# Softmax times V: transposed probabilities copied out of PSUM two row blocks at a time, and the store of the second last pass moved between the loads of the last head

## Chip, cores, metric

One core of one Trainium2 chip. The metric is the device time of one execution in microseconds (us); lower is better. Medians are over the runs named.

## The reference

```python
batch, n_heads, seq, head_dim = 8, 12, 1024, 64        # float32
attn = np.exp(scores - scores.max(-1, keepdims=True))
attn = attn / (attn.sum(-1, keepdims=True) + 1e-8)
return np.matmul(attn, v)
```

There are 96 heads. Each has 4 MB of scores and needs 1024 x 1024 exponentials.

## The kernel before

The loop takes four heads (k = 0 to 3) per pass, 24 passes. A head is 8 row blocks (r) of 128 rows. For each two row blocks ScalarE takes exponentials (the kernel does not subtract the row's maximum first). Then, for each row block, TensorE transposes eight 128x128 squares into one PSUM tile, VectorE copies the tile to SBUF, and TensorE makes eight products with V and a column of ones. VectorE divides by the sums.

```python
EB = 2; LAG = 2; AHEAD = 4                   # row blocks per exponential, lag of products, heads per pass
p_bufs   = buffers(sb_pool, 8, [P, EB, SK], FP16, "p_nat")
pt_bufs  = buffers(sb_pool, 4, [P, SK], FP16, "pt")
psT_bufs = buffers(ps_pool, 4, [P, SK], FP16, "psT")
# ... cut ...
def heads(n0):
    for k in range(AHEAD):
        # ... cut: for k == 0, spread_v of this head ...
        for r in range(R):
            # ... cut: exponential of two row blocks when r is even (one by one at the very end) ...
            psT = take(psT_bufs)
            for c in range(C):
                nc.tensor.transpose(out=psT[:, c*P:(c+1)*P], in_=p_row[:, c//L, c%L, :], identity=order16[:])
            pt = take(pt_bufs)
            copy = nc.vector.tensor_copy(out=pt[:], in_=psT[:])
            # ... cut: on every other r spread_v of the next head; at r == R-1 load_next ...
            pending.append((n0, k, r, pt, st))
            if len(pending) > LAG:
                finish(pending.pop(0))       # eight products; then reciprocal and scaling (normalise)
    while pending:
        finish(pending.pop(0))
    cast_v()
    last(n0)                                 # loads of later heads and the store of heads 2 and 3
# in last(), for the pass before the last:
load(AHEAD - 2, BH - 2, (4, 4))
load(AHEAD - 1, BH - 1, (2, 2, 2, 1, 1))     # the very last head, in five parts
store(n0, AHEAD - T)
```

## Time and profile before

| | before |
|---|---|
| median of the first three runs | 1066.23 us |
| span in the profile | 1064.1 us |
| occupied: 16 DMA engines / VectorE / ScalarE / TensorE | 99.2% / 74% / 69% / 69% |
| DMA rate, 20 to 1000 us | 432 GB/s |
| last store issued / landed | 1059.60 / 1062.24 us |

The DMA engines are occupied nearly all the time and no compute engine above 74%, so over most of the run the data sets the time. Only near the end, as the loads run out, does compute count.

### The profile page before, as it was taken

To read this page: it belongs to the slowest core of one execution; us is meant where nothing else is said; L and a number is where in the kernel's file an instruction comes from. 1 tells how busy PE (TensorE), PEld (TensorE's weight loads), DVE (VectorE), ACT (ScalarE), POOL (GpSimd) and SP (SyncE) were. 2 spreads that over 40 slices of the span, in tenths; PEclk is the share of its full clock that TensorE was granted. 3 is DMA by queue.
4 is the path that set the end of the run, shared out by engine and by line. 5 is a ranking of instruction groups with operands and counts; after the bars stand their busy time and mean duration, and the time that the engine had idled before them with its cause. 6 is when DMAs were issued, how large, how long until landed. Compare 5 with 4: busy or idle time off the path is not lost.

```text
span 1064.1 us, 32213 instructions
## 1 busy us (share of the span) xinstructions
PE 734.8 (69%) x12288; PEld 682.6 (64%) x12288; DVE 786.6 (74%) x1589; ACT 735.8 (69%) x432; POOL 48.0 (5%) x31
## 2 busy tenths in 40 slices
PE   2766766767766667677686776767666777667675
PEld 2765765667666667666575665767665667666575
DVE  3776867868768777677786776868768687686777
ACT  3766776666767668586676866667766668676685
POOL 0000000000000000000000000000000000000000
PEclk9888888878889888888888888878889787897989
DMA  9999999999999999999999999999999999999995
GB/s 394 432 420 434 425 433 434 433 434 433 433 432 432 424 439 432 434 429 427 434 431 436 434 432 434 431 435 422 439 432 434 430 426 435 434 432 427 439 427 233
DMA packets 24915, 453.05 MB, mean 426 GB/s; under 512 B 2768, under 2 KB 2768, under 8 KB 9168
## 3 DMA queue, kind: packets, MB, share of 16 engines
q1 hardware_dynamic: 24912, 453.00, 99.2%
q8 instruction: 3, 0.05, 0.0%
HBM read 436.21 MB, written 25.17 MB: 434 GB/s over the span
## 4 chain that ended last, share of the span: by engine, by line
DMA 78%; ACT 13%; PEld 4%; PE 3%; DVE 1%; issue 1%; SPq 0%; ACTq 0%; DVEq 0%
DMA s_nat<-in_scores_dram 78%; ACT p_nat L255 13%; PEld L267 2%; PE psT L267 2%; PEld L145 1%; DVE pt L273 1%; PE psO_whole L145 1%; PE psO L145 1%; SPq L185 0%; DVE out_sb L129 0%; ACTq L255 0%; SPq L197 0%; DVE recip L124 0%; ACTq L227 0%; DVE vones L208 0%
## 5 line engine op out<-in xcount | busy, mean ns | idle before, releaser
L255 ACT ACTIVATE p_nat<-s_nat 128x2048 f16<-128x2048 f32 (+1 forms) x408 | 705.0, 1800 | 226.7 <-DMA s_nat<-in_scores_dram 200.9
L267 PE MATMUL psT<-order,p_nat 128*128 128x128 f16 x6144 | 578.0, 247 | 263.9 <-ACT p_nat L255 256.9
L273 DVE COPY pt<-psT 128x1024 f16<-128x1024 f16 x768 | 515.6, 687 | 199.9 <-PE L267 121.3
L267 PEld LDWEIGHTS <-p_nat 128*128 128x128 f16 x6144 | 449.9, 123 | 291.1 <-ACT p_nat L255 288.8
L145 PEld LDWEIGHTS <-pt 128*128 128x128 f16 x6144 | 303.1, 108 | 84.4 <-DVE pt L273 81.4
L145 PE MATMUL psO<-vones,pt 128*128 128x65 f16 x3072 | 177.9, 202 | 56.2 <-DVE pt L273 52.6
L145 PE MATMUL psO_whole<-vones,pt 128*128 128x65 f16 x3072 | 190.3, 212 | 3.3 <-DVE pt L273 2.9
L208 DVE COPY vones<-v_half 32x512 f16<-32x512 f16 x384 | 109.4, 285 | 23.1 <-POOL v_half L204 6.0
L255 ACT ACT_TABLE_LOAD x24 | 30.8, 1283 | 89.7 <-DMA s_nat<-in_scores_dram 81.7
L204 POOL CAST v_half<-v_sb 128x2048 f16<-128x2048 f32 x25 | 47.3, 1893 | 1002.2 <-DVE vones L208 957.1
L129 DVE TENSOR_TENSOR out_sb<-psO,recip 64x256 f32<-64x256 f32 x192 | 81.2, 423 | 6.1
L129 DVE TENSOR_TENSOR out_sb<-psO_whole,recip 64x512 f32<-64x512 f32 x96 | 66.1, 688 | 3.7 <-DMA out_dram<-out_sb 0.7
L124 DVE RECIPROCAL recip<-psO 128x4 f32<-128x4 f32 x96 | 17.1, 179 | 34.2 <-PE psO L145 17.8
L124 DVE RECIPROCAL recip<-psO_whole 128x8 f32<-128x8 f32 x48 | 9.7, 203 | 4.8 <-PE psT L267 4.0
L71 DVE MEMSET vones<- 128x16 f16 x4 | 0.2, 72 | 0.8 <-PEq L309 0.8
L62 DVE CAST order<-ident 128x128 f16<-128x128 f32 x1 | 0.2, 227 | 0.4 <-POOL ident masks.py:199 0.4
masks.py:199 POOL TENSOR_SCALAR_AFFINE_SELECT ident<-ident 128x128 f32<-128x128 f32 x1 | 0.3, 292 | 0.1
masks.py:197 POOL MEMSET ident<- 128x128 f32 x1 | 0.2, 204 | 0.3 <-POOLq L309 0.3
L309 POOL MEMSET const-float32-0.0<- 128x1 f32 x1 | 0.1, 98 | 0.2 <-issue 0.2
L309 POOL MEMSET const-bfloat16-1.0<- 128x1 bf16 x1 | 0.1, 102 | 0.0
L309 POOL MEMSET const-uint8-127<- 128x1 uint8 x1 | 0.1, 102 | 0.0
L309 POOL MEMSET const-float32-1.0<- 128x1 f32 x1 | 0.1, 98 | 0.0
## 6 DMA issues: line engine op xcount, KB each, us to landing
s_nat<-in_scores_dram SPq DMA_DIRECT2D x96, 4096.0 KB, 35.9
v_sb<-in_v_dram SPq DMA_DIRECT2D x24, 1024.0 KB, 33.0
out_dram<-out_sb SPq DMA_DIRECT2D x48, 512.0 KB, 27.0
s_nat<-in_scores_dram SPq DMA_DIRECT2D x2, 2048.0 KB, 32.8
s_nat<-in_scores_dram SPq DMA_DIRECT2D x3, 1024.0 KB, 32.6
s_nat<-in_scores_dram SPq DMA_DIRECT2D x2, 512.0 KB
```

Of the source, the lines that this page charges most:

```text
L62: nc.vector.tensor_copy(out=order16[:].rearrange("p (t j) -> p t j", t=T), in_=ident32[:].rearrange("p (j t) -> p t j", t=T),)
L71: nc.vector.memset(vo[:, :, D : D + 2], 1.0)
L124: nc.vector.reciprocal(out=recip, in_=psO[:, :, :, D : D + 1])
L129: nc.vector.tensor_tensor(out=rows.rearrange("j (b g) d -> j b g d", g=G), in0=psO[part, :, :, 0:D], in1=recip[part].to_broadcast([W, last ...
L145: nc.tensor.matmul(out=bank[:, g * M : (g + 1) * M], lhsT=pt[:, c * P : (c + 1) * P], rhs=st["vones"][:, c, 0:M], start=(c == 0), stop=(c ...
L204: nc.gpsimd.tensor_copy(out=v_half[:], in_=v_sb[:])
L208: copy = nc.vector.tensor_copy(out=vones_bufs[k][s * Q : (s + 1) * Q, :, 0:D].rearrange("i (h l) d -> i h l d", l=L), in_=v_half[k * Q : ( ...
L255: nc.scalar.activation(out=p_nat[:, g : g + rows, :].rearrange("p r (x v) -> p x r v", v=Q * L), in_=s_bufs[k][:, r + g : r + g + rows, :] ...
L267: nc.tensor.transpose(out=psT[:, c * P : (c + 1) * P], in_=p_row[:, c // L, c % L, :], identity=order16[:],)
L273: copy = nc.vector.tensor_copy(out=pt[:], in_=psT[:])
L309: nc = _bacc.Bacc("TRN2", target_bir_lowering=False, num_devices=1)
```

## The change

The intent is to halve the number of VectorE copies (a single one took 687 ns in the kernel before), and to have the store of the pass before land early, so that the last pass does not wait for it.

```diff
-    pt_bufs = buffers(sb_pool, 4, [P, SK], FP16, "pt")
+    pt_bufs = buffers(sb_pool, 2, [P, EB, SK], FP16, "pt")
-    psT_bufs = buffers(ps_pool, 4, [P, SK], FP16, "psT")
+    psT_bufs = buffers(ps_pool, 2, [P, EB, SK], FP16, "psT")
...
                 load(AHEAD - 2, BH - 2, (4, 4))
-                load(AHEAD - 1, BH - 1, (2, 2, 2, 1, 1))
+                load(AHEAD - 1, BH - 1, (4,))
                 store(n0, AHEAD - T)
+                load(AHEAD - 1, BH - 1, (2, 1, 1), 4)
...
                 if r % EB == 0:
-                    p_nat = take(p_bufs)
+                    p_nat, psT, pt = take(p_bufs), take(psT_bufs), take(pt_bufs)
...
-                        out=psT[:, c * P : (c + 1) * P],
+                        out=psT[:, r % EB, c * P : (c + 1) * P],
...
+                if k < AHEAD - 2 and r == R - 1:
+                    load_next(k, n0)
+                if r % EB < EB - 1:
+                    continue
                 copy = nc.vector.tensor_copy(out=pt[:], in_=psT[:])
-                if k < AHEAD - 1 and r % (R // S) == 0:
-                    spread_v(k + 1, r // (R // S), copy)
-                if r == R - 1:
-                    load_next(k, n0)
-                pending.append((n0, k, r, pt, st))
-                if len(pending) > LAG:
+                if k < AHEAD - 1:
+                    spread_v(k + 1, r // EB, copy)
+                pending.extend((n0, k, r - EB + 1 + e, pt[:, e], st) for e in range(EB))
+                while len(pending) > LAG:
                     finish(pending.pop(0))
```

More of the change, by code (lines that the diff above doesn't have):

```diff
@@ L179, in apart, with load @@
         )
-    def load(k, n, parts=(R,), **cond):
-        r = 0
+    def load(k, n, parts=(R,), r=0, **cond):
         for rows in parts:
@@ L264, in heads @@
                 p_row = p_nat[:, r % EB, :].rearrange("p (h q l) -> p h l q", q=P, l=L)
-                psT = take(psT_bufs)
                 for c in range(C):
                     nc.tensor.transpose(
-                        out=psT[:, c * P : (c + 1) * P],
+                        out=psT[:, r % EB, c * P : (c + 1) * P],
                         in_=p_row[:, c // L, c % L, :],
@@ L271, in heads @@
                     )
-                pt = take(pt_bufs)
+                if k < AHEAD - 2 and r == R - 1:
+                    load_next(k, n0)
+                if r % EB < EB - 1:
+                    continue
                 copy = nc.vector.tensor_copy(out=pt[:], in_=psT[:])
-                if k < AHEAD - 1 and r % (R // S) == 0:
-                    spread_v(k + 1, r // (R // S), copy)
-                if r == R - 1:
-                    load_next(k, n0)
-                pending.append((n0, k, r, pt, st))
-                if len(pending) > LAG:
+                if k < AHEAD - 1:
+                    spread_v(k + 1, r // EB, copy)
+                pending.extend((n0, k, r - EB + 1 + e, pt[:, e], st) for e in range(EB))
+                while len(pending) > LAG:
                     finish(pending.pop(0))
@@ L284, in heads @@
         last(n0)
-    assert BH % AHEAD == 0 and BH >= 2 * AHEAD and SK == Q * S * C
+    assert R // EB == S and BH % AHEAD == 0 and BH >= 2 * AHEAD and SK == Q * S * C
     load_v(0)
```

## The prediction

> **What bounds the kernel now.** I read the page's busy shares first, then the slices and the DMA section, then the chain, then the last 20 us in the timeline of VectorE.
>
> ```profile
> PE 734.8 (69%) x12288; PEld 682.6 (64%) x12288; DVE 786.6 (74%) x1589; ACT 735.8 (69%) x432; POOL 48.0 (5%) x31
> ...
> DMA  9999999999999999999999999999999999999995
> ...
> q1 hardware_dynamic: 24912, 453.00, 99.2%
> ...
> DMA 78%; ACT 13%; PEld 4%; PE 3%; DVE 1%; issue 1%; SPq 0%; ACTq 0%; DVEq 0%
> ```
>
> No compute engine is above 74%, while the 16 DMA engines are occupied for 99.2% of the span; only the last slice falls short. A table of windows gives a DMA share of 1.00 and 432 GB/s from 20 to 1000 us. One head moves 453 MB / 96 = 4.72 MB, which is 10.9 us at 432 GB/s. VectorE needs 786.6 / 96 = 8.2 us per head, PE and ScalarE 7.7 each. So VectorE has 2.7 us to spare on every head. The chain agrees: 78% of it is the load of scores. The only places where compute can set the time are the first loads, which the change leaves alone, and the end, after the DMA stream runs dry.
>
> ```profile
> 1048.73 1.89 DVE L273 COPY pt<-psT 128x1024 f16<-128x1024 f16 x3
> 1050.54 0.20 DVE L124 RECIPROCAL recip<-psO_whole 128x8 f32<-128x8 f32 x1
> 1050.70 0.69 DVE L273 COPY pt<-psT 128x1024 f16<-128x1024 f16 x1
> 1052.14 1.41 DVE L129 TENSOR_TENSOR out_sb<-psO_whole,recip 64x512 f32<-64x512 f32 x2 [0.74 <-DMA out_dram<-out_sb]
> 1053.57 1.89 DVE L273 COPY pt<-psT 128x1024 f16<-128x1024 f16 x3
> 1055.38 0.17 DVE L124 RECIPROCAL recip<-psO 128x4 f32<-128x4 f32 x1
> 1055.47 0.66 DVE L273 COPY pt<-psT 128x1024 f16<-128x1024 f16 x1
> 1056.16 0.88 DVE L129 TENSOR_TENSOR out_sb<-psO,recip 64x256 f32<-64x256 f32 x2
> 1057.07 0.69 DVE L273 COPY pt<-psT 128x1024 f16<-128x1024 f16 x1
> 1058.48 0.18 DVE L124 RECIPROCAL recip<-psO 128x4 f32<-128x4 f32 x1 [0.72 <-PE psO L145]
> 1058.70 0.88 DVE L129 TENSOR_TENSOR out_sb<-psO,recip 64x256 f32<-64x256 f32 x2
> ```
>
> This is the end. VectorE is nearly solid from 1048.7 to 1059.6, with two holes: 0.74 us waiting for a store, and 0.72 us waiting for the last product. The first hole is what the second half of the change aims at: normalising the head before the last overwrites an output buffer whose previous store is queued behind every load, so it lands only at 1052.1. The second belongs to the last link (last copy, eight products, reciprocal, scaling). The final store is then issued at 1059.60, lands 2.6 us later, and the span ends at 1064.1.
>
> ScalarE also matters here. In its timeline the last head's exponentials start at 1044.62 (rows 0,1), 1046.42 (2,3), 1048.40 (4,5), 1050.22 (6) and about 1051.2 (7), ending at 1052.22. Rows 4,5 were waiting for data:
>
> ```profile
> L185 SPq DMA_DIRECT2D s_nat<-in_scores_dram x1: 328/328/328, 1015.0 to 1015.0; - x1
> DMA to landing us min/median/max: 33.3/33.3/33.3
> ```
>
> Issued at 1015.0, landed at 1048.3, used at 1048.40. The transfers before it, read alike, landed at 1043.3 (rows 0,1) and 1045.8 (rows 2,3): 2.5 us per megabyte.
>
> [...] with the store last in the queue landing last; so a store placed earlier pushes back the loads behind it by its own transfer time. [...] The trace has 687 ns per copy and 0.65 us from start to start back to back[...] VectorE is saturated only in the last 10 us.
>
> **The change part by part.**
>
> *Copies.* 768 copies of 687 ns become 384 of twice the size. [...] 384 x 1.221 = 469 us against 515.6 in the by-form groups, and VectorE falls from 786.6 to about 740 us (70%). On the path in the steady state: nothing, because it adds to a slack of 2.7 us per head. PSUM stays at four row blocks, now as two pairs. The instruction order on PE becomes 16 transposes of the next pair, then 16 products of the pair before, so a copy has a whole group of products and transposes to hide behind. Coarser hand-off does not starve PE either: 7.7 us of work per head, and 10.9 us to do it in. Later release of a score buffer would cost nothing, since a load has some 36 us from issue to landing, more than three heads of queue.
>
> *Loads and store at the end.* The last head came as 2,2,2,1,1 rows, then the store. Now it is 4 rows, the store, then 2,1,1. The bytes are the same, so the last byte of the stream stays where it is, near 1051.7. But the pieces move: 0.5 MB of store is 1.25 us, half of the 2.5 above. Rows 0 to 3 land together at 1045.8 (rows 0,1 thus 2.5 us later than before); the store at about 1047.1 (it was 1052.1); rows 4,5 at 1049.55; row 6 at about 1050.8; row 7 at about 1052.1.
>
> *The end, step by step (us, on the old trace's axis).* ScalarE: rows 0,1 from 1045.93 (before: 1044.62), then 1.81 apart: 1047.75 for rows 2,3, 1049.64 for rows 4,5 (after their landing), 1051.45 for row 6, 1052.45 for row 7, ending at 1053.45, 1.2 later than before. VectorE, with 1.0 us for 16 transposes and the order that the built program has:
> - copy of rows 0,1: 1047.83 + 1.1 = 1048.95 to 1050.17;
> - reciprocal and scaling of the head before, 0.20 + 1.41, with no wait for the store: to 1051.8;
> - copy of rows 2,3 to 1053.0 (transposed long before);
> - copy of rows 4,5 to 1054.2;
> - reciprocal and scaling of the first bank, 0.18 + 0.88: to 1055.3;
> - copy of rows 6,7, whose transposes follow the products of rows 2,3 and end near 1054.8: 1055.35 to 1056.57;
> - 16 products instead of 8 before the end: 0.64 + 8 more at 0.03 = 0.90, to 1057.5;
> - reciprocal and scaling, 1.1: to 1058.63.
>
> Before, this point was 1059.58. The sum: four copies of 1.22 for eight of 0.67 saves 0.5; the store's wait saves 0.74; the later arrival of rows 0,1 makes VectorE begin this stretch some 0.3 later than its own backlog would, and the final 16 products cost 0.26 more. Together about -0.9 to -1.0. The final store and the close (4.5 us) are unchanged. So 1066.23 - 1.0 = **1065.2 us**, 0.1% faster.
>
> **The rivals.**
>
> *The store before the last rows simply delays the end.* If the last row's arrival bound the end, everything after ScalarE's last exponential (7.4 us in the trace, 1052.22 to 1059.60) would shift by 1.2, and the time would be about 1067.4. For it: rows 4,5 were waited for. Against it: in the trace VectorE, not ScalarE, is the solid engine after 1048.7, and when the last exponential ended it still had five copies and two scalings to do. I give it one chance in six, in part or whole.
>
> *VectorE was a hidden bound, and 46 us less of it shortens the run.* Its busiest slices show 8 tenths. If each head were gated by it, up to 0.5 us x 96 = 46 us, 4%, would come off. Against it: the DMA share of 1.00 through 980 us; time can only fall if DMA falls, and no byte is removed. Under 1%.
>
> *Two PSUM tiles turn into a new wait in every pair.* Four single buffers let PE run up to four blocks ahead; two pairs let it start the third pair only when the first is copied. If transposes and copies alternated strictly, a pair would cost about 16 transposes (1.3 at the granted clock of 0.84) plus 1.22 copy plus 0.29, then products 0.9: 3.7 us, 14.8 per head, above 10.9, and the run would be near 1400. The order of instructions rules out the strict form, because copies of one tile run beside transposes into the other. A partial form raises PE's idle time, and still has some 2 us per head to hide in. About 1% for anything over 2%.
>
> **Range and chances.** The repeats of before span 0.36 us. My step sum carries perhaps 0.6 either way (copy duration over two banks, order of arrival), the delay rival pulls up to 1.2 above before, and the DMA stream itself may drift by a tenth of a per cent between two programs. Hence 1064.0 to 1066.8. Two per cent is 21 us; nothing off the DMA path can reach it. Faster 0.01, same 0.98, slower 0.01.
>
> **What would show each step right or wrong.** Right: a DMA share of 1.00 and 432 GB/s from 20 to 1000 us; 384 copies of about 1.22 us; VectorE near 740 us; no wait of line 129 on the output store; rows 4,5 landing near 1049.5; ScalarE ending near 1053.4 and the last store issued near 1058.6. Wrong: a copy of 1.3 us or more (banks cost extra); a wait of transposes on copies worth tens of us with DMA share below 0.99 (the third rival); the last store issued after 1060 (the first rival). The prediction as a whole is wrong if the DMA stream has gaps that it did not have.

The terms as named are -0.5, -0.74, +0.3 and +0.26, the list of steps came to 1058.63 against 1059.58, and the forecast to -1.0, that is 1065.2 us. But the 1.22 us for a pair copy, in the steps and in the first term, and with it the 469 us of all copies and the 46 us that VectorE would save, was the estimate; measured later were 1225 ns and 469.7 us. That the store, last in the queue, lands last is in the trace: issued at 1031.34, it landed at 1052.1, and the exponential of the last rows had begun at about 1051.2. Placed earlier, in the changed kernel, it landed 1.39 us after rows 0 to 3 (1047.44 and 1046.05), and rows 4,5 landed at 1049.87 instead of 1048.3. The 0.03 us for one product more agrees with the median distance between the starts of products in the trace of the kernel before (33 ns from 1030 to 1060 us). The 1.3 us for 16 transposes was the estimate too; in the changed kernel (mean granted clock 0.87) groups of 16 took 1.24 us on average.

## The result

The changed kernel took 1066.66 us (median of 4, 1066.62 to 1067.30) against 1066.26 for the kernel before (4 runs on the same chip). The ratio is 1.0006 with a 95% interval of 0.9988 to 1.0023. A ratio here is the mean time of one kernel's fast runs over that of the other's of the same rounds, so not quite the ratio of the medians. A gain of 1.0 us was predicted; 0.4 us was lost. The page of the changed kernel, lines as in the first fence of the prediction:

```profile
PE 714.7 (67%) x12288; PEld 665.3 (62%) x12288; DVE 746.0 (70%) x1205; ACT 735.9 (69%) x432; POOL 48.1 (5%) x31
...
DMA  9999999999999999999999999999999999999995
...
q1 hardware_dynamic: 24768, 453.00, 99.1%
...
DMA 78%; ACT 13%; issue 3%; PE 2%; DVE 2%; ACTq 1%; PEld 0%; SPq 0%; DVEq 0%
...
L275 DVE COPY pt<-psT 128x2048 f16<-128x2048 f16 x384 | 469.7, 1225 | 250.9 <-PE L145 102.7
```

The DMA stream is what it was. VectorE (DVE) has 384 instructions fewer and is occupied 40.6 us less, none of which shows in the time. So the answer lies in the end. VectorE's timeline there (start, duration, and in brackets the idle time before and what ended it):

```profile
1048.63 1.23 DVE L275 COPY pt<-psT 128x2048 f16<-128x2048 f16 x1 [0.26 <-PE L145]
1049.89 0.29 DVE L207 COPY vones<-v_half 32x512 f16<-32x512 f16 x1
1050.55 1.23 DVE L275 COPY pt<-psT 128x2048 f16<-128x2048 f16 x1 [0.37 <-PE psO_whole L145]
1051.69 0.20 DVE L124 RECIPROCAL recip<-psO_whole 128x8 f32<-128x8 f32 x1
1051.92 1.41 DVE L129 TENSOR_TENSOR out_sb<-psO_whole,recip 64x512 f32<-64x512 f32 x2
1053.36 2.36 DVE L275 COPY pt<-psT 128x2048 f16<-128x2048 f16 x2
1055.79 0.18 DVE L124 RECIPROCAL recip<-psO 128x4 f32<-128x4 f32 x1
1056.00 0.88 DVE L129 TENSOR_TENSOR out_sb<-psO,recip 64x256 f32<-64x256 f32 x2
1056.91 1.23 DVE L275 COPY pt<-psT 128x2048 f16<-128x2048 f16 x1
1059.34 0.18 DVE L124 RECIPROCAL recip<-psO 128x4 f32<-128x4 f32 x1 [1.20 <-PE psO L145]
1059.55 0.88 DVE L129 TENSOR_TENSOR out_sb<-psO,recip 64x256 f32<-64x256 f32 x2
```

The store's wait of 0.74 us is gone from line 129, as intended. In its place copies wait for TensorE (0.26, 0.37, and more further up), and the last reciprocal waits 1.20 us instead of 0.72. The last store is issued at 1060.46 instead of 1059.60. Of these 0.86 us, 0.2 are the stream of this one execution: head 1 of the last pass is first used at 1030.21 instead of 1030.01.

What are the copies waiting for? TensorE's timeline beside them:

```profile
1048.62 1.06 PE L266 MATMUL psT<-order,p_nat 128*128 128x128 f16 x16
1049.91 0.68 PE L145 MATMUL psO_whole<-vones,pt 128*128 128x65 f16 x16 [0.23 <-DVE pt L275]
1050.43 1.06 PE L266 MATMUL psT<-order,p_nat 128*128 128x128 f16 x16
```

The copy that starts at 1050.55 needs the 16 transposes from 1048.62, whose last ends at 1049.68 by this view. VectorE is free at 1050.18. So why not then? The trace also records semaphore updates, and those of TensorE's semaphore number 24,579 for 12,288 transposes and products and 12,288 weight loads: one for each, and three more. I call these completion marks. In all of the changed kernel no two of them are less than 29 ns apart, and 92% of the gaps are 30 ns or less; in the kernel before the numbers are 29 and 91%. Two row blocks are 16 transposes and 16 products, each with a weight load: 64 marks, and 64 x 30 ns = 1.92 us. TensorE itself takes about 1.6 us for them (from the first product at 1049.91 to the end of the last transpose at 1051.49), so the marks fall behind. Counting them back from the end of the trace, the last mark before 1050.55 belongs to one of the last transposes of that group, begun 1.1 us earlier (two of the three marks without an instruction record come after the last product, so this can be off by 0.06 us). The same spacing shows in VectorE's own timeline, further up in the last pass:

```profile
1029.86 1.23 DVE L275 COPY pt<-psT 128x2048 f16<-128x2048 f16 x1 [0.82 <-PE L145]
1031.12 0.28 DVE L207 COPY vones<-v_half 32x512 f16<-32x512 f16 x1
1031.78 1.22 DVE L275 COPY pt<-psT 128x2048 f16<-128x2048 f16 x1 [0.38 <-PE psO_whole L145]
1033.04 0.29 DVE L207 COPY vones<-v_half 32x512 f16<-32x512 f16 x1
1033.70 1.22 DVE L275 COPY pt<-psT 128x2048 f16<-128x2048 f16 x1 [0.38 <-PE psO_whole L145]
```

From 1029.86 to 1031.78 to 1033.70 are 1.92 us each, though a copy and the spread behind it take only 1.5. (The releaser named, a product, is the instruction whose modelled end lies nearest; by the count it is a transpose.) The mark of that transpose comes about 0.9 us after its modelled end.

### The profile page after: what moved, and what is told of

The parts are those of the page before. It is cut to its first block, busy times and chain, and to the rows that moved or that the text cites. A ratio compares the mean times of both kernels' runs of the same rounds, so it can differ in the third digit from the quotient of the medians.

```text
span 1064.9 us, 30721 instructions
## 1 busy us (share of the span) xinstructions
PE 714.7 (67%) x12288; PEld 665.3 (62%) x12288; DVE 746.0 (70%) x1205; ACT 735.9 (69%) x432; POOL 48.1 (5%) x31
## 4 chain that ended last, share of the span: by engine, by line
DMA 78%; ACT 13%; issue 3%; PE 2%; DVE 2%; ACTq 1%; PEld 0%; SPq 0%; DVEq 0%
DMA s_nat<-in_scores_dram 78%; ACT p_nat L255 13%; DVE pt L275 1%; PE psT L266 1%; ACTq L255 1%; PE psO L145 1%; PE psO_whole L145 1%; ACTq L226 0%; ACTq L292 0%; PEld L145 0%; SPq L184 0%; PEld L266 0%; ACTq L320 0%; DVE out_sb L129 0%; SPq L196 0%
## 5 line engine op out<-in xcount | busy, mean ns | idle before, releaser
L266 PE MATMUL psT<-order,p_nat 128*128 128x128 f16 x6144 | 498.0, 245 | 263.2 <-ACT p_nat L255 258.9
L275 DVE COPY pt<-psT 128x2048 f16<-128x2048 f16 x384 | 469.7, 1225 | 250.9 <-PE L145 102.7
L266 PEld LDWEIGHTS <-p_nat 128*128 128x128 f16 x6144 | 435.5, 123 | 287.5 <-ACT p_nat L255 287.0
L145 PEld LDWEIGHTS <-pt 128*128 128x128 f16 x6144 | 253.5, 105 | 105.9 <-DVE pt L275 97.6
L145 PE MATMUL psO<-vones,pt 128*128 128x65 f16 x3072 | 139.7, 200 | 71.6 <-DVE pt L275 70.4
L145 PE MATMUL psO_whole<-vones,pt 128*128 128x65 f16 x3072 | 149.4, 206 | 9.4 <-DVE pt L275 8.8
## 6 DMA issues: line engine op xcount, KB each, us to landing
s_nat<-in_scores_dram SPq DMA_DIRECT2D x1, 1024.0 KB, 26.2
```

Of the source, the lines that this page charges most:

```text
L145: nc.tensor.matmul(out=bank[:, g * M : (g + 1) * M], lhsT=pt[:, c * P : (c + 1) * P], rhs=st["vones"][:, c, 0:M], start=(c == 0), stop=(c ...
L266: nc.tensor.transpose(out=psT[:, r % EB, c * P : (c + 1) * P], in_=p_row[:, c // L, c % L, :], identity=order16[:],)
```

## The experiments

**Theory W**: in the last heads, where compute sets the end, TensorE's completion marks leave too little room for a coarse hand-off. A pair copy has to wait for 32 transposing marks where a single one waits for 16, and after the last pair 32 product marks are left instead of 16. **Rival D**: the store in front of the last rows delays their landing, and with it the end. Later rivals are named where they arise. "Span of the end" below is the time from the first exponential of head 1 in the last pass to the issue of the last store; before: 29.60 us, with VectorE occupied for 26.64 of it.

All times are medians of 5 runs, with the kernel before at 1066.2 to 1066.3 (9 runs) each time. Each kernel's own 95% interval is about plus or minus 0.14%, or 1.5 us. So a difference of half a microsecond rests on the runs' ranges and on the traces.

### The two halves apart

```diff
 # after_again: the changed kernel, no edit
 # copies_only: the changed kernel with
-                load(AHEAD - 1, BH - 1, (4,))
+                load(AHEAD - 1, BH - 1, (2, 2, 2, 1, 1))
                 store(n0, AHEAD - T)
-                load(AHEAD - 1, BH - 1, (2, 1, 1), 4)
 # order_only: the kernel before with
-                load(AHEAD - 1, BH - 1, (2, 2, 2, 1, 1))
+                load(AHEAD - 1, BH - 1, (4,))
                 store(n0, AHEAD - T)
+                load(AHEAD - 1, BH - 1, (2, 1, 1), 4)
```

> The changed kernel once more, as the mark for the others on the same chip. Theory W (pairs of rows make VectorE wait for TensorE's completions in the last pass): 0.3 to 0.7 us above the kernel before, VectorE idle about 5.8 us between the first spread of the last pass and the end (before: 3.4). Theory D (the store in front of the last rows delays the end): the same time, so this run alone tells nothing apart.

> The pair copies with the old order of loads and store. Theory W: the loss is here, so this is the slowest of the four, 0.8 to 1.6 us above the kernel before, with waits of copies on TensorE of 2 us or more in the last pass and 1.2 us before the last reciprocal. Theory D: the copies are the good half, so 0.5 to 1.0 us below the kernel before.

> Single copies with the store between the parts of the last head. Theory W: the store's wait of 0.74 us goes and nothing else changes much, since VectorE is behind anyway when the rows land: 0.4 to 0.8 us below the kernel before. Theory D: the last rows land 1.25 us later, so up to 1.2 us above the kernel before.

| | median | range | ratio | span of the end | VectorE occupied in it |
|---|---|---|---|---|---|
| after_again | 1066.53 | 1066.23 to 1067.40 | 1.0003 | 29.93 | 26.26 |
| copies_only | 1067.60 | 1067.20 to 1067.72 | 1.0012 | 30.80 | 26.14 |
| order_only | 1065.70 | 1065.50 to 1066.24 | 0.9997 | 29.23 | 26.90 |

Both came out as W has it and against D. The pair copies alone cost 1.4 us, and none of their runs is as fast as the slowest of before (1066.61). The order alone is 0.5 us below; its runs overlap those of before, so the size is uncertain, but a loss of 1.2 us, as D had it, is out: its slowest run took 1066.24, and its last store is issued at 1059.31 instead of 1059.60. Waits of VectorE by releaser, from the first exponential of head 1 on (total, times, longest), first the changed kernel, in the run of the result:

```profile
DVE recip L124 <- PE psO L145: 1.2, 1, 1.2
DVE pt L275 <- PE psO_whole L145: 1.1, 3, 0.4
DVE pt L275 <- PE L145: 1.1, 2, 0.8
```

and order_only:

```profile
DVE recip L124 <- PE psO L145: 0.7, 1, 0.7
DVE pt L273 <- PE psO_whole L145: 0.3, 1, 0.3
DVE pt L273 <- PE psO L145: 0.2, 1, 0.2
```

The 0.8 in the first view lies before the window (the copy that follows it, at 1029.86, is still running when the window begins) and does not count. The balance of the table: from order_only to after_again the pairs save 0.64 us of VectorE's work in three heads (26.90 to 26.26), and its idle time, short gaps included, grows by 1.34 (2.33 to 3.67). The spans differ by the 0.70 between.

### Only the last pair copied singly

```diff
 # last_single: the changed kernel with
+                if k == AHEAD - 1 and r >= R - EB:
+                    nc.vector.tensor_copy(out=pt[:, r % EB], in_=psT[:, r % EB])
+                    pending.append((n0, k, r, pt[:, r % EB], st))
+                    while len(pending) > LAG:
+                        finish(pending.pop(0))
+                    continue
```

> The changed kernel, but the last two row blocks of each pass's last head are copied one by one. Theory W: after the last copy only 8 products (16 TensorE instructions) are left instead of 16, and the last copy is 0.69 instead of 1.22 us: the wait before the last reciprocal falls from 1.20 to 0.72, and the time by 0.5 to 1.0 us against the changed kernel, to about 0.2 to 0.6 below the kernel before. Theory D: the time is set by the landing of the last rows and what follows it, so a gain of at most 0.5.

It took 1066.85 us (1066.11 to 1067.51; ratio 1.0005): no gain. The wait itself did as expected, yet the reciprocal starts where it starts in after_again (1059.15 in both):

```profile
1056.11 0.69 DVE L274 COPY pt<-psT 128x1024 f16<-128x1024 f16 x1 [0.30 <-PE psO L145]
1056.83 0.88 DVE L129 TENSOR_TENSOR out_sb<-psO,recip 64x256 f32<-64x256 f32 x2
1057.74 0.69 DVE L274 COPY pt<-psT 128x1024 f16<-128x1024 f16 x1
1059.15 0.18 DVE L124 RECIPROCAL recip<-psO 128x4 f32<-128x4 f32 x1 [0.72 <-PE psO L145]
```

The wait fell from 1.20 to 0.72 us, but the built program puts the copy of row 6 in front of the scaling of the first bank, where it waits 0.30 for TensorE, and the two copies take 0.15 us more than one. That gives the 0.48 back. My expectation had left out the order of VectorE's instructions.

### Marks, or TensorE's work?

The marks (**W1**) and TensorE's working time (**W2**) are two forms of theory W. One experiment doubles the work of each product at the same number of instructions, the other takes instructions away.

```diff
 # wide: the changed kernel; V tiles hold one block more, and for heads 2 and 3 of a pass
-                out=bank[:, g * M : (g + 1) * M],
+                out=bank[:, g * M : (g + 2) * M],
-                rhs=st["vones"][:, c, 0:M],
+                rhs=st["vones"][:, c : c + 2, 0:M],
 # half: the changed kernel; for heads 2 and 3 (wrong result on purpose)
-        for c in range(C):
+        for c in range(0, C, 2):
```

> The changed kernel with every product of the third and fourth head of a pass twice as wide (130 columns instead of 65, the second half unused; results stay right). Same number of TensorE instructions, more time in each. Theory W1 (TensorE's completion marks, 30 ns apart, 64 per pair, set the pace of the last pass, 1.92 us per pair): no change, within 0.4 us of the changed kernel; copies in the third head still 1.92 us apart, last reciprocal still waits 1.20 us. Theory W2 (TensorE's working time sets the pace): 16 products take about 0.4 us more per pair, so pairs 2.2 us or more apart, the last wait about 1.6 us, and the end 2 to 3 us later.

> The changed kernel with only every other product in the third and fourth head of a pass (wrong result on purpose). 16 TensorE instructions fewer per pair. W1: the marks of a pair fall from 1.92 to 1.44 us, so the waits of copies on TensorE in those heads nearly vanish, the last reciprocal waits 1.20 - 0.48 = 0.72 us, and the time falls by 1.0 to 1.8 us against the changed kernel. W2: 8 products fewer are 0.26 us less, so the last wait is 0.94, and the time falls by 0.3 to 0.8.

The kernel half took 1065.05 us (ratio 0.9988), 1.5 us below after_again, inside W1's range and outside W2's. It carries its own control, since only heads 2 and 3 were thinned: in head 0 its copies start at 1027.53, 1029.45 and 1031.37, still 1.92 us apart, and in head 2 and at the start of head 3:

```profile
1046.49 1.23 DVE L276 COPY pt<-psT 128x2048 f16<-128x2048 f16 x1
1047.75 0.29 DVE L208 COPY vones<-v_half 32x512 f16<-32x512 f16 x1
1048.07 1.22 DVE L276 COPY pt<-psT 128x2048 f16<-128x2048 f16 x1
1049.32 0.29 DVE L208 COPY vones<-v_half 32x512 f16<-32x512 f16 x1
1049.65 1.23 DVE L276 COPY pt<-psT 128x2048 f16<-128x2048 f16 x1
```

They follow 1.58 us apart with no wait: VectorE's own pace. In the changed kernel the last two of these three waited 0.26 and 0.37 us. The expected last wait of 0.72 could not be read, because in this build the last copy stands in front of a scaling that covers the wait.

The kernel wide took 1072.25 us (ratio 1.0056), far outside both forms. Its span of the end was 30.08 us, that of the changed kernel (30.24, 29.93), so the end was not slower. What was slower was everything before: the first exponential of the last pass came at 1027.22 instead of 1021.80. The next runs show why.

### An early table load, and an accident of placement

ScalarE loads its table in each pass (24 loads of 1.28 us in the kernel before), and only when the first scores have landed: of the 89.7 us for which it is idle before them, 81.7 end with a landing of scores. If the whole last pass were bound by compute, moving this load out of the way should help.

```diff
 # order_warm: order_only with, after_warm: the changed kernel with
+    warm = const_pool.tile([P, 2], FP32, name="warm")
+    nc.vector.memset(warm[:], 0.0)
...
+        nc.scalar.activation(out=warm[:, 1:2], in_=warm[:, 0:1], func=EXP)     # start of each pass
```

> Single copies, new order of loads and store, and one exponential of a constant at the start of each pass, so that the table load of 1.28 us no longer stands between the landing of the first head's scores and its exponentials. If the whole last pass is bound by compute from that landing on (theory W), the end comes 0.8 to 1.3 us earlier than with the order alone: about 1.3 to 1.8 us below the kernel before. If the end is set by the landing of the last rows (theory D), nothing: 0.5 below.

> The changed kernel with the same early table load. Theory W: 0.8 to 1.3 us below the changed kernel, so 0.4 to 1.0 us below the kernel before, and still about 0.9 us behind the same thing with single copies. Theory D: as the changed kernel.

They took 1072.28 and 1072.53 us (ratios 1.0057 and 1.0061), like wide. What the three share is that a small tile in front moves all later buffers: the score buffers no longer start at 21504 (42 x 512) but 32 bytes (the two warm kernels) or 128 bytes (wide) past a multiple of 512. **Theory A** takes that for the cause. It was tested by padding the three tiles to a multiple of 512, in order_warm_pad, after_warm_pad and wide_pad, and by shifting the kernel before:

```diff
 # order_warm_pad, after_warm_pad
-    warm = const_pool.tile([P, 2], FP32, name="warm")
+    warm = const_pool.tile([P, 128], FP32, name="warm")
 # wide_pad: wide with, ahead of the V tiles
+    pad = const_pool.tile([P, 96], FP32, name="pad")
 # before_shift: the kernel before with
+    pad = const_pool.tile([P, 8], FP32, name="pad")        # 32 bytes, never read
```

> The single copies with the new order and the early table load, but the added constant is 512 bytes per partition instead of 32, so that the score buffers start again at a multiple of 512 bytes as in the kernel before (in the runs wide, order_warm and after_warm they started at 128 or 32 bytes past one). Theory A (those runs were slow because the loads write to shifted buffers): the stream is back at the old rate, the last pass begins near 1020.4 us, and the early table load shows what it is worth: 0.8 to 1.3 us below order_only, so about 1064.4 to 1064.9. Theory A-not (the early exponential or the loop made them slow): 1072 again.

> The changed kernel with the same padded early table load. Theory A with theory W: 0.8 to 1.3 us below the changed kernel, about 1065.2 to 1065.8, and so still 0.7 to 1.0 us behind order_warm_pad. Theory A-not: 1072 again.

> The doubled products again, with the score buffers back at a multiple of 512 bytes. Theories A and W1: within 0.4 us of the changed kernel, about 1066.2 to 1067.0. W2 (TensorE's working time): 2 to 3 us above it. Theory A-not: 1072 again.

> The kernel before with one unused constant of 32 bytes per partition, nothing else: all later buffers lie 32 bytes further. Theory A: 5 to 7 us above the kernel before, with a DMA rate of 431 instead of 432 to 434 GB/s all the way. Theory A-not: the time of the kernel before.

| | median | ratio | span of the end |
|---|---|---|---|
| before_shift | 1072.93 | 1.0061 | 30.18 |
| wide_pad | 1066.89 | 1.0003 | 29.99 |
| order_warm_pad | 1065.79 | 0.9996 | 29.18 |
| after_warm_pad | 1066.88 | 1.0004 | 29.91 |

Theory A holds: 32 unused bytes per partition cost 6.6 us, and padding takes the loss away in all three. The slices of the DMA rate (GB/s, 40 slices) of before_shift; most are at 430 or 431, where those of the kernel before are mostly at 432 to 434 (from 20 to 1000 us, 430 against 432):

```profile
GB/s 395 432 419 432 424 436 431 431 431 430 431 431 431 430 430 427 434 431 431 431 430 431 426 434 431 430 431 430 431 431 431 431 431 431 429 431 431 431 428 172
```

From 100 to 900 us the mean packet takes 1213.1 ns in the kernel before and 1216.1 in before_shift for scores (32 KB), 309.0 and 314.4 for V (8 KB), 159.3 and 160.0 for stores (4 KB). The shift moves all of these buffers, and no run separates them. By what mechanism the start of a buffer acts was not shown either.

With that out of the way, wide_pad settles W1 against W2. Its products take 1.08 us per pair instead of 0.68, and TensorE has hardly a gap left; without a wait it begins pairs 1.81 us apart (1048.19 and 1050.00):

```profile
1048.19 1.08 PE L149 MATMUL psO_whole<-vones,pt 128*128 128x130 f16 x16
1049.11 1.06 PE L270 MATMUL psT<-order,p_nat 128*128 128x128 f16 x16
1050.00 1.08 PE L149 MATMUL psO_whole<-vones,pt 128*128 128x130 f16 x16
```

Yet VectorE's copies come as before:

```profile
1048.49 1.23 DVE L279 COPY pt<-psT 128x2048 f16<-128x2048 f16 x1 [0.29 <-PE psO_whole L149]
...
1050.41 1.22 DVE L279 COPY pt<-psT 128x2048 f16<-128x2048 f16 x1 [0.37 <-PE psO_whole L149]
...
1059.25 0.18 DVE L127 RECIPROCAL recip<-psO 128x4 f32<-128x4 f32 x1 [1.23 <-PE psO L149]
```

Again 1.92 us apart, with the same waits to 0.03 us, and the same time as the changed kernel within 0.4 us. Sixty per cent more working time in the products changed nothing, so the pace is that of the marks.

The early table load itself was a miss: 1065.79 with it and 1065.70 without for single copies, 1066.88 and 1066.53 for pairs. ScalarE's timeline in order_warm_pad shows where the time went:

```profile
1020.39 7.31 ACT L258 ACTIVATE p_nat<-s_nat 128x2048 f16<-128x2048 f32 x4 [1.95 <-DMA s_nat<-in_scores_dram]
1030.08 14.78 ACT L258 ACTIVATE p_nat<-s_nat 128x2048 f16<-128x2048 f32 x8 [2.38 <-DMA s_nat<-in_scores_dram]
```

Head 0 is begun 1.3 us earlier than in order_only, but head 1 lands at 1030.0 as ever, and ScalarE waits 2.38 us for it instead of 1.08. So the stretch in which compute sets the end begins with head 1 and holds three heads, not four.

### Are pairs slow in themselves?

What was left open is whether the marks are why pairs lose, or whether a coarser hand-off loses anyway. Taking a quarter of TensorE's instructions from both versions, in all heads, tells this apart (wrong results on purpose). It takes away working time too, but that wide_pad has excluded as the pace.

```diff
 # half_all_pairs: the changed kernel; half_all_single: order_only
-        for c in range(C):
+        for c in range(0, C, 2):
```

> The changed kernel with every other product left out in all heads (wrong result on purpose): 48 TensorE instructions per pair of row blocks instead of 64, so 1.44 us of marks per pair. W1: in the last three heads the waits of copies on TensorE vanish and VectorE alone sets the pace (7.8 us per head), so this beats half_all_single by 0.4 to 1.2 us, the reverse of the true kernels, where pairs lose 0.9 us. Rival (a pair is slower whatever TensorE does, because its copy starts only when both rows are there): pairs still lose 0.5 us or more.

> The single copies with the new order of loads and store, with every other product left out in all heads (wrong result on purpose). VectorE alone sets the pace here too, at 8.3 us per head. W1: 0.4 to 1.2 us behind half_all_pairs, and only some 0.3 to 0.6 us below order_only, which hardly waited for TensorE. Rival: 0.5 us or more ahead of half_all_pairs.

They took 1065.06 (1064.81 to 1065.51) and 1065.23 us (1064.84 to 1065.47). The deficit of the pairs, 0.8 us in the true kernels (1066.53 against 1065.70), is gone; pairs are now 0.2 ahead, which the runs do not resolve. The rival expected them 0.5 or more behind and falls. W1 has the direction, but not the size of 0.4 to 1.2. The traces say why: VectorE is occupied only 0.36 us less with pairs in the span of the end (26.04 against 26.40), and is idle 0.21 us longer (2.34 against 2.13), which is the longer wait before the last reciprocal (0.72 against 0.51). A caution: in these builds, as in half, two copies stand at other places in VectorE's order than in the changed kernel.

## Why the prediction was wrong

**The bound, the copies' duration, the landings: right.** The DMA rate is 432 GB/s from 20 to 1000 us in both kernels. The 384 copies take 1225 ns (predicted 1221), and VectorE comes to 746 us (about 740). Rows 0 to 3 landed at 1046.05, the store at 1047.44, rows 4,5 at 1049.87, and ScalarE ended at 1053.79. That is 0.2 to 0.35 later than predicted, of which 0.2 are the later stream of this execution.

**"Right: no wait of line 129 on the output store": right, with the expected size.** The order alone gave 0.5 us (0.37 in the span of the end) where the term was 0.74 less a later arrival of 0.3. The first rival, that the store delays the end, is out.

**"Copy of rows 0,1: 1048.95": the step that failed.** It started at 1050.55, 1.6 us later. I took VectorE to be done with the head before by then, and to be "saturated only in the last 10 us". It was not, in either kernel. In the kernel before it was occupied for 9.60 of the 10 us from 1040 to 1050. The three copies at 1048.73 in the prediction's second fence begin with row 7 of the head before (the last head has eight, counted from the end); rows 0 and 1 follow at 1049.34 and 1049.94. So 0.4 of the 1.6 us is a line misread, and the term for a later arrival was counted from a backlog that ended too early. The other 1.2, of which 0.2 are the later stream, came with the pairs: VectorE copied that head's last pair from 1048.63 to 1049.86, because ever since head 1 landed the copies had been waiting for marks. The prediction put 7.7 us of TensorE work per head beside 10.9 us of data, and took the rest for slack. But in the last three heads the data is there sooner than TensorE's marks, and 4 x 1.92 = 7.68 us per head is then a floor that no busy share shows. Single copies live under the same floor: in the 29.60 us of the kernel before, 872 marks at 30 ns fill 26.2, and beyond those 30 ns the marks pause for 2.3 us in all. In order_only they pause for 2.0, in after_again for 2.6, at the places where TensorE waits for VectorE to copy a pair. So the coarse hand-off does not raise the floor; it lets the marks run dry for longer.

**"16 products cost 0.26 more": too small.** The term was 8 products at 0.03 us. The wait before the last reciprocal grew by 0.48 (0.72 to 1.20), which is 16 more instructions, weight loads included, at 30 ns.

**"Four copies for eight saves 0.5" in the last head: too large.** It compared 1.22 with twice 0.67, in the very place where single copies run back to back. Three take 1.89 us and one 0.69, so each further one adds 0.60 (the prediction read 0.65 from start to start); two pairs take 2.36, so the second adds 1.13. VectorE's measured saving is 0.64 us over three heads, or 0.2 per head.

**The sum.** The four terms named (-0.5, -0.74, +0.3, +0.26) make -0.68, not -0.9 to -1.0. The larger gain came from the list of steps (1059.58 to 1058.63), whose first copy stands too early. That 1066.66 still lies within the stated range is luck: its upper end was set for the first rival. The sign set for that rival, a last store after 1060, came true as well (1060.46), but order_only shows that the rival was not the cause.

**The third rival was the one that came, in a small form.** The prediction saw that two tiles could turn into a wait in every pair, and dismissed it because 2 us per head of slack would hide it. That is true of 93 heads and not of the last three. The reason is also not the one named there: in the lines above the transposes follow the products without a wait of their own for a PSUM tile; what was late was the news of their completion, about 0.9 us after the modelled end of the transpose in "The result".

**In sum**, from order_only to the changed kernel: 0.64 us of VectorE's work saved and 1.34 us of idle time added in the span of the end, which is the difference of 0.70 between the two spans.

**What stays open.** Every run quoted was recorded in the same way, so whether the marks would come faster unrecorded is not shown. No kernel with fewer marks for the same work was tried. The gain of the order alone, 0.5 us, lies within the interval of a single comparison. It is the fastest correct version tried, 0.05% below the kernel before.

## What to carry to other kernels

In this kernel, bound by its loads (DMA share 1.00 from 20 to 1000 us), 40.6 us less of VectorE's work did not show in the time; the change acted only from the landing of the first head that compute could not keep up with, at 1030 of 1064 us. Where loads set the time, find that point first, and take the costs from that stretch alone. A larger instruction that reads another engine's output also waits for more of it (here 64 marks, 1.92 us, for each pair copy, and 1.20 us instead of 0.72 after the last one): count what the consumer must wait for before and after, in instructions as well as in working time, and count what is left after the last one. When an added tile changes the time far from where it is used (here 32 bytes per partition, 6.6 us), look at where the other buffers have moved before reading anything else into it.
